# Branch sums, norms, residuals and gated products kept in PSUM banks, and a residual's bias added inside the feed-forward

## The chip, the cores and the metric

The kernel runs on one core of a Trainium2 chip. The metric is device time in microseconds (us) of one execution, with the median of several runs as the figure. A core has five engines that run in parallel, each with its own queue of instructions in a fixed order: PE (matrix products), VectorE (DVE in the profile), ScalarE (ACT), GpSimd (POOL) and SyncE (SP, which here only issues transfers). An instruction may wait on semaphores for others; whatever stands behind it on its engine then waits too. PE writes its products into PSUM, which the kernel uses as eight banks of 128 x 512 fp32; every other tile lies in SBUF.

## The reference

Two transformer blocks on 256 tokens of 1024 channels, all in fp32:

```
h = layer_norm(x)
proj = h @ w_in + b_in                      # q, k, v of two attentions, gates ga and gb
y_na  = neighbourhood_attention(...) @ w_branch_na
y_swa = windowed_gqa_with_sink(...) @ w_branch_swa
mixed = sigmoid(ga) * y_na + sigmoid(gb) * y_swa
h = layer_norm(ALPHA * h + mixed @ w_out + b_out)
u = square(relu(h @ w_ff1 + b_ff1))
h = layer_norm(ALPHA * h + u @ w_ff2 + b_ff2)
# second block, two layers
for layer in range(2):
    m = pool_mixer(rms_norm(x)) if layer == 0 else swa_sink_attention(rms_norm(x)) @ w_o
    x = x + rms_norm(m, mix_post_g)
    g, v = split(conv3(rms_norm(x) @ ffn_w_in))
    x = x + rms_norm((gelu(g) * v) @ ffn_w_out, ffn_post_g)
```

The pool mixer takes causal trailing means over 2, 4, 8 and 16 tokens minus the token itself, and a linear map per channel group. The convolution is causal, depthwise and three tokens wide.

## The kernel before

Every fp32 operand of a product is a pair of parts, a high one (the value in PE's fp32r format) and a low one (the rest). A product is three matmuls: high by high, low by high, high by low (`mm3`, L369). Weights stream through the core once, as chunks of 128 x 1024 (512 KB): SP loads a chunk into one of four `wraw` tiles, ACT writes its high part `whi` (L131), DVE its low part `wlo` (L141), and when DVE has done so SP may issue the next load. All 261 low parts of this kind are on DVE.

PSUM has two groups of four banks that rotate, `bank_a` and `bank_b`. A unit (`unit_a`) makes 256 output channels for all 256 tokens in two halves (m = 0 and 1); each half is a run of matmuls into the first 256 columns of the next `bank_a`, and an epilogue reads it. So the fourth half after a given one writes to the same bank, and PE must wait until the bank's last reader is done. `Acc` holds sums over many chunks in the four `bank_b` (two blocks of 128 tokens by two halves of 512 channels).

The order on every engine is the order in which the Python code issues instructions; nothing reorders it. The places that the change touches, in order of time:

- The branch stage (160 to 185 us). `y_swa` is made in four units of two halves, 12 matmuls a half. The epilogue `swa_epi` runs for each half i: DVE gated sum (L770, reads the bank), DVE `mix` (L772), ACT high part `mixh` (L775), a DVE `wlo` of the weights, DVE low part `mixl` (L777). Then comes the product with `w_out`.
- The first layer norms (`post_ln`, L290 to L284). DVE adds the residual to the bank and writes SBUF (`scr` is the name of those tiles), takes statistics there, centres, and scales.
- The entry of the feed-forward (205 to 237 us). The norm of tokens 128 to 255 is turned to feature-major and split (`to_fm`, `xl`), while PE runs three units for the first 128 tokens (`Tm.run`), whose outputs ACT copies (`tmc`). Right behind the second `xl`, DVE makes `h1 = ALPHA * h1 + b_ff2` for both token blocks (L907). `bff2` is one of four vectors that POOL loads then (L219).
- The feed-forward's loop, units 3 to 15: `ur` is relu (ACT, L889) and square (DVE, L890), `uh` and `ul` its parts; each turn also adds two chunks to the second product in `bank_b`.
- The pool stage (386 to 403 us). `pool_mm(0)` makes the mixer's output for tokens 0 to 127 in two `bank_b`. `resid_g` (L327) multiplies it by a gain, `sq_half` (ACT, L302) squares and sums it, `rms_rstd` (DVE `ve`, L307, then POOL) gives the inverse root, and `resid_add` (L331) adds the scaled product to X. In between `a_scale` (DVE, L952) scales the pooling matrix for tokens 128 to 255, on which `pool_fm(1)` on PE waits.
- The conv-GLU blocks (units 0 to 21, twice). For each half ACT and DVE make the convolution from the bank in an SBUF tile `cv` (L1085, L1086, L1088). After the second half ACT makes gelu in place in SBUF (L1092), DVE the product (L1093), and `split_out` the parts `ah` (ACT) and `al` (DVE). Units 0 to 2 are run ahead and finished between units 3, 4 and 5, through `bank_b`. From unit 6 on each turn also adds a chunk to the block's output. The residual chain behind a block is `resid_g`, `rms_rstd` and `resid_add` again.

Of the kernel before, what the change touches and what calls it, by code (L numbers as in the profile page):

```python
# [177 lines left out]
def model(tc, x_in, wts, bvec, cols_in, const_in, nab_in, pos_in, out):  # L178
    nc = tc.nc
    from contextlib import ExitStack  # L180
    with ExitStack() as top:
# [95 lines left out]
        def ln_centre(y, mr, g, q):  # L277
            s = HALF[q]
            nc.vector.scalar_tensor_tensor(out=y[:, s], in0=y[:, s], scalar=mr[0], in1=g[:, s],
                                           op0=ALU.subtract, op1=ALU.mult)  # L280

        def ln_out(y, mr, b, h, q):
            s = HALF[q]
            nc.vector.scalar_tensor_tensor(out=h[:, s], in0=y[:, s], scalar=mr[1], in1=b[:, s],  # L284
                                           op0=ALU.mult, op1=ALU.add)
# [1236 lines left out]
```

## Time and profile before

| | us |
|---|---|
| median of 3 runs | 884.81 (884.22 to 885.89) |
| the profiled execution | 879.9 |
| its span (first to last instruction) | 878.1 |
| PE busy | 836.4 (95%) |
| DVE busy | 631.0 (72%) |
| ACT busy | 492.0 (56%) |
| POOL busy | 146.0 (17%) |

The profile is of one execution, 879.9 us, of which 1.8 us lie around the span of 878.1. PE is busy in 95% of the span; its granted clock was 0.997 of full speed. Of the chain that ended last PE has 68%, DVE 16%, ACT 7%, 4% are issue and 3% transfers. A row of a timeline gives start, length and operation, and in brackets the idle time of that engine before it with what ended it. [...]

### The profile page before, as it was taken

How to read it: one execution, taken by the hardware profiler on the slowest of the kernel's cores; microseconds unless marked ns; L12 is line 12 of the kernel's file. 1: busy time of each engine (PE TensorE's matmuls, PEld its weight loads, DVE VectorE, ACT ScalarE, POOL GpSimd, SP SyncE). 2: the span in 40 equal slices, each digit the busy share in tenths (PEclk: the TensorE clock that was granted, in tenths of full speed). 3: DMA queues.
4: the chain of work that ended last, by engine and by line, in shares of the span. 5: the costliest groups of instructions: out<-in, count | busy, mean ns of one | idle time of the engine just before them, and what ended most of it. 6: DMA issues, size and time to landing. Idle time of an engine off the chain costs nothing.

```text
span 878.1 us, 15167 instructions
## 1 busy us (share of the span) xinstructions
PE 836.4 (95%) x5872; PEld 754.9 (86%) x5872; DVE 631.0 (72%) x1055; ACT 492.0 (56%) x905; POOL 146.0 (17%) x160
## 2 busy tenths in 40 slices
PE   4999999999899999898999999999999999999997
PEld 3878899979788999788999999988776999999995
DVE  4675684787838755777799777765696679977772
ACT  3464765544526555445677565465786566765551
POOL 0003000004999000311000000056720000000000
PEclk9999999999999999999999999999999999999999
DMA  7683364537636865533547655534153455766531
GB/s 265 201 305 106 137 196 135 174 124 241 217 97 199 295 227 192 177 111 121 178 149 268 194 183 205 191 117 137 53 189 120 145 192 186 250 213 208 175 121 48
DMA packets 43899, 154.61 MB, mean 176 GB/s; under 512 B 5010, under 2 KB 5906, under 8 KB 43827
## 3 DMA queue, kind: packets, MB, share of 16 engines
q1 hardware_dynamic: 41616, 146.90, 49.1%
q0 software_dynamic: 1632, 5.93, 2.1%
q8 instruction: 46, 0.75, 0.3%
q10 hardware_dynamic: 578, 0.82, 0.3%
q14 instruction: 27, 0.21, 0.1%
HBM read 152.58 MB, written 1.05 MB: 175 GB/s over the span
## 4 chain that ended last, share of the span: by engine, by line
PE 68%; DVE 16%; ACT 7%; issue 4%; DMA 3%; POOL 0%; SPq 0%; DVEq 0%; POOLq 0%; ACTq 0%
PE bank_a L369 36%; PE bank_b L369 24%; DVE wlo L141 7%; PE bank_a L424 4%; ACT whi L131 3%; DMA wraw<-wts_dram 2%; DVE p L1262 1%; DVE p L698 1%; ACT p L1274 1%; PE bank_a L348 1%; PE bank_a L720 1%; PE bank_b L709 1%; ACT scr L302 1%; DMA v<-bvec_dram 1%; PE bank_b L657 1%
## 5 line engine op out<-in xcount | busy, mean ns | idle before, releaser
L141 DVE TENSOR_TENSOR wlo<-wraw,whi 128x1024 fp32r<-128x1024 f32 x261 | 320.7, 1257 | 83.0 <-ACT whi L131 82.5
L369 PE MATMUL bank_a<-xh,whi 128*128 128x256 f32 x1056 | 295.9, 280 | 1.9 <-DVE cv L1088 1.7
L369 PE MATMUL bank_a<-xh,wlo 128*128 128x256 f32 x1056 | 292.7, 277 | 0.7 <-DVE wlo L141 0.5
L369 PE MATMUL bank_a<-xl,whi 128*128 128x256 f32 x1056 | 292.5, 277 | 0.0
L131 ACT ACTIVATE whi<-wraw 128x1024 fp32r<-128x1024 f32 x261 | 264.9, 1050 | 31.8 <-DMA wraw<-wts_dram 25.0
L369 PEld LDWEIGHTS bank_a<-xh,whi 128*128 128x128 f32 x1056 | 198.4, 188 | 7.3 <-ACT whi L131 2.7
L369 PEld LDWEIGHTS bank_a<-xl,whi 128*128 128x128 f32 x1056 | 198.7, 188 | 1.7
L369 PEld LDWEIGHTS bank_a<-xh,wlo 128*128 128x128 f32 x1056 | 198.4, 188 | 1.3 <-DVE wlo L141 1.3
L1085 ACT ACTIVATE cv<-bank_a,cols 128x256 f32<-128x256 f32 x76 | 41.9, 559 | 78.8 <-PE bank_a L369 78.8
L266 POOL TENSOR_TENSOR rstd<-ve,neghalf 128x1 f32<-128x1 f32 x22 | 13.4, 611 | 400.8 <-DVE ve L307 247.9
L369 PE MATMUL bank_b<-wlo,ah 128*128 128x512 f32 x176 | 69.3, 394 | 0.0
L369 PE MATMUL bank_b<-whi,al 128*128 128x512 f32 x176 | 69.0, 392 | 0.0
L369 PE MATMUL bank_b<-whi,ah 128*128 128x512 f32 x176 | 68.5, 389 | 0.0
L1086 DVE SCALAR_TENSOR_TENSOR cv<-bank_a,cols,cv 128x255 f32<-128x255 f32 x76 | 36.5, 481 | 41.9 <-ACT cv L1085 41.6
L869 POOL TENSOR_SCALAR wraw<-wraw,cols 128x256 f32<-128x256 f32 x28 | 29.7, 1079 | 166.1 <-DMA wraw<-wts_dram 162.4
L369 PE MATMUL bank_b<-whi,uh 128*128 128x512 f32 x128 | 50.3, 393 | 3.2 <-ACT uh L338 3.2
L369 PE MATMUL bank_b<-whi,ul 128*128 128x512 f32 x128 | 50.7, 396 | 2.5 <-DVE ul L339 2.5
L369 PE MATMUL bank_b<-wlo,uh 128*128 128x512 f32 x128 | 50.3, 393 | 0.0
L369 PEld LDWEIGHTS bank_b<-wlo,ah 128*128 128x128 f32 x176 | 33.1, 188 | 6.6
L1088 DVE SCALAR_TENSOR_TENSOR cv<-bank_a,cols,cv 128x254 f32<-128x254 f32 x76 | 36.6, 482 | 2.7
L369 PEld LDWEIGHTS bank_b<-whi,al 128*128 128x128 f32 x176 | 33.1, 188 | 6.3
L369 PEld LDWEIGHTS bank_b<-whi,ah 128*128 128x128 f32 x176 | 33.0, 188 | 6.0
(199 smaller groups left out, 1290.9 us busy)
## 6 DMA issues: line engine op xcount, KB each, us to landing
wraw<-wts_dram SPq DMA_DIRECT2D x268, 512.0 KB, 4.5
v<-bvec_dram POOLq DMA_DIRECT2D x10, 512.0 KB, 5.4
v<-bvec_dram SPq DMA_DIRECT2D x4, 512.0 KB, 7.1
nab<-nab_dram SPq DMA_DIRECT2D x4, 384.0 KB, 5.7
poolA<-const_dram POOLq DMA_DIRECT2D x1, 544.0 KB, 8.0
scr<-x_dram SPq DMA_DIRECT2D x2, 256.0 KB, 2.8
scr<-x_dram SPq DMA_DIRECT2D x1, 512.0 KB, 11.1
out_dram<-X SPq DMA_DIRECT2D x2, 256.0 KB, 2.1
```

The costliest lines, as they stand in the source:

```text
L131: self.nc.scalar.activation(out=hi, in_=r, func=AF.Copy)
L141: (eng or self.nc.vector).tensor_tensor(out=lo, in0=r, in1=hi.bitcast(F32), op=ALU.subtract)
L266: nc.gpsimd.tensor_tensor(out=r, in0=v, in1=neghalf, op=ALU.pow)
L302: nc.scalar.activation(out=junk[:, HALF[q if into is None else into]], in_=src, func=AF.Square, scale=1.0 / 32.0, accum_out=ss[:, q:q + 1])
L348: nc.tensor.transpose(out=b[:, j * P:(j + 1) * P], in_=h[:, k * P:(k + 1) * P], identity=ident)
L369: nc.tensor.matmul(o, lhsT=l, rhs=r, start=start and i == 0, stop=stop and i == 2)
L424: nc.tensor.matmul(o[:, :256], lhsT=self.kx(k)[b][:, t * P:(t + 1) * P], rhs=self.cs[u][k // 4][a][:, k % 4, :], start=i == 0 and k == 0, ...
L657: nc.tensor.matmul(s[e][:, j * T:(j + 1) * T], lhsT=q[r, j * P:(j + 1) * P], rhs=k[r, :], start=True, stop=True)
L869: nc.gpsimd.tensor_scalar(out=d, in0=d, scalar1=g, scalar2=None, op0=ALU.mult)
L1085: nc.scalar.activation(out=v, in_=o[:, :T], func=AF.Identity, scale=col(c + 2), bias=col(c + 3))
L1086: nc.vector.scalar_tensor_tensor(out=v[:, 1:T], in0=o[:, 0:T - 1], scalar=col(c + 1), in1=v[:, 1:T], op0=ALU.mult, op1=ALU.add)
L1088: nc.vector.scalar_tensor_tensor(out=v[:, 2:T], in0=o[:, 0:T - 2], scalar=col(c), in1=v[:, 2:T], op0=ALU.mult, op1=ALU.add)
```

## The change

Nothing of the arithmetic and no matmul is changed. Values that DVE and ACT kept in SBUF stay in the PSUM bank where PE left them, written over in place:

- `swa_epi` makes the gated sum and the mix in the half's `bank_a` columns; the low part `mixl` of half i is issued behind the sums of half i + 1.
- The layer norms behind `w_out` and behind the feed-forward add the residual, take statistics and centre in `bank_b`; only the last step writes SBUF. (The very first norm stays in SBUF.)
- `resid_g` writes its product over the `bank_b` it reads, and `resid_add` reads it there. In the pool stage the first `resid_g` stands in the code behind the squares instead of before them.
- The gelu and the gated product of a conv-GLU unit are made in columns 256 to 511 of the second half's `bank_a`, and `split_out` reads them there.
- `h1 = ALPHA * h1 + b_ff2` moves into units 12 and 13 of the feed-forward's loop, and the load of `bff2` to behind that of the pooling matrix on POOL's queue.

In the title's words "all low parts on VectorE" nothing differs from the kernel before.

```diff
...
-            nc.vector.scalar_tensor_tensor(out=y[:, s], in0=y[:, s], scalar=mr[0], in1=g[:, s],
+            nc.vector.scalar_tensor_tensor(out=y[q], in0=y[q], scalar=mr[0], in1=g[:, HALF[q]],
                                            op0=ALU.subtract, op1=ALU.mult)
...
-        def ln_stats(y, st, q, add=None, resid=None):
-            s = HALF[q]
-            if add is not None:
-                nc.vector.tensor_tensor(out=y[:, s], in0=add[q], in1=resid[:, s], op=ALU.add)
-            nc.vector.bn_stats(out=st[:, q, :], in_=y[:, s])
+        def ln_stats(y, st, q, resid=None):
+
+            if resid is not None:
+                nc.vector.tensor_tensor(out=y[q], in0=y[q], in1=resid[:, HALF[q]], op=ALU.add)
+            nc.vector.bn_stats(out=st[:, q, :], in_=y[q])
...
-        def resid_g(halves, g, junk, q):
+        def resid_g(halves, g, q):
+
+            nc.vector.tensor_tensor(out=halves[q], in0=halves[q], in1=g[:, HALF[q]], op=ALU.mult)
+
+        def resid_add(r, x, halves, q):
             s = HALF[q]
-            nc.vector.tensor_tensor(out=junk[:, s], in0=halves[q], in1=g[:, s], op=ALU.mult)
-
-        def resid_add(r, x, junk, q):
-            s = HALF[q]
-            nc.vector.scalar_tensor_tensor(out=x[:, s], in0=junk[:, s], scalar=r, in1=x[:, s],
+            nc.vector.scalar_tensor_tensor(out=x[:, s], in0=halves[q], scalar=r, in1=x[:, s],
                                            op0=ALU.mult, op1=ALU.add)
...
             def epi(m, o):
                 i = 2 * u + m
                 g, z = gate["gb", i], gate["ga", i]
-                nc.vector.scalar_tensor_tensor(out=g, in0=g, scalar=1.0, in1=o[:, :T], op0=ALU.add, op1=ALU.mult)
-                s = rot(apool, [P, T], F32, "mix", "mix", 2)
-                nc.vector.tensor_tensor(out=s, in0=g, in1=z, op=ALU.add)
+                s = o[:, :T]
+                nc.vector.scalar_tensor_tensor(out=s, in0=g, scalar=1.0, in1=s, op0=ALU.add, op1=ALU.mult)
+                nc.vector.tensor_tensor(out=s, in0=s, in1=z, op=ALU.add)
                 hi = rot(gpool, [P, T], F32R, "ga", "mixh", 8)
                 lo = rot(gpool, [P, T], F32R, "gb", "mixl", 8)
                 nc.scalar.activation(out=hi, in_=s, func=AF.Copy, scale=0.5)
                 mixed[i] = (hi, lo)
-                return [lambda: nc.vector.scalar_tensor_tensor(out=lo, in0=s, scalar=0.5, in1=hi.bitcast(F32),
-                                                               op0=ALU.mult, op1=ALU.subtract)]
+                if i:
+                    mix_low.pop()()
+                mix_low.append(lambda: nc.vector.scalar_tensor_tensor(
+                    out=lo, in0=s, scalar=0.5, in1=hi.bitcast(F32), op0=ALU.mult, op1=ALU.subtract))
             return epi
 
+        mix_low = []
         for u in range(4):
             unit_a(lambda k: att[4 + k], swa_epi(u), 4, ahead=1)
+        mix_low.pop()()
 
 
         ctx_x.close()
...
         tm = Tm(kx, 3, fpool)
         post_ln(acc, 1, x_t[1], g1, b1, h1[1])
         pscale = vec(V_PSCALE)
-        bff2 = vec(V_BFF2)
         g2 = vec(V_G2)
         b2 = vec(V_B2)
         tm.run(0)
         to_fm(h1[1], xT1, 1)
-        for t in range(2):
-            nc.vector.scalar_tensor_tensor(out=h1[t], in0=h1[t], scalar=ALPHA, in1=bff2, op0=ALU.mult, op1=ALU.add)
         tm.run(1)
         rope_angles()
         ctx_p = ExitStack()
         ppool = ctx_p.enter_context(tc.tile_pool(name="mixer", bufs=1, side="right"))
         poolA = ppool.tile([P, 4, N_POOL // 4], F32, name="poolA")
         nc.gpsimd.dma_start(out=poolA.rearrange("p a c -> p (a c)"), in_=const_in[:, K_POOL:K_POOL + N_POOL])
+        bff2 = vec(V_BFF2)
         mixpost0 = vec(V_MIXPOST0, None, late, "bx", 1)
         acc = Acc(32)
         for u in range(3, 16):
...
             unit_a(kx, ff1_epi(u))
+            if u in (12, 13):
+                nc.vector.scalar_tensor_tensor(out=h1[u - 12], in0=h1[u - 12], scalar=ALPHA, in1=bff2, op0=ALU.mult,
+                                               op1=ALU.add)
...
             sq_half(X[1][:, HALF[q]], j1, ss2[1], q)
         nc.scalar.activation(out=cb, in_=fb[1][:, :P], func=AF.Copy)
-        resid_g(accp.b[0], mixpost0, j0, 0)
         for q in range(2):
             sq_half(accp.b[0][q], j0, ss0, q, 1)
+        resid_g(accp.b[0], mixpost0, 0)
         lows = W.highs(2)
         r1 = rms_rstd(ss2[1])
         a_scale(1, r1)
         r0 = rms_rstd(ss0)
-        resid_g(accp.b[0], mixpost0, j0, 1)
+        resid_g(accp.b[0], mixpost0, 1)
         fb = pool_fm(1, cb)
         lows[0]()
         for q in range(2):
-            resid_add(r0, X[0], j0, q)
+            resid_add(r0, X[0], accp.b[0], q)
...
                     if m == 1:
-                        nc.scalar.activation(out=got[0], in_=got[0], func=AF.Gelu_apprx_tanh)
-                        nc.vector.tensor_tensor(out=v, in0=v, in1=got[0], op=ALU.mult)
+                        y = o[:, T:2 * T]
+                        nc.scalar.activation(out=y, in_=got[0], func=AF.Gelu_apprx_tanh)
+                        nc.vector.tensor_tensor(out=y, in0=v, in1=y, op=ALU.mult)
                         hi = rot(fp, [P, T], F32R, "ah", "ah", 8)
                         lo = rot(fp, [P, T], F32R, "al", "al", 8)
                         a_t[u] = (hi, lo)
-                        return [lambda: split_out(v, hi, lo)]
+                        return [lambda: split_out(y, hi, lo)]
...
```

The remaining places only pass the bank instead of the SBUF tile.

On DVE in the branch stage the kernel before has, from half 0 on (`gb` and `ga` are the gates, `mixl` the low part):

```order
L770 SCALAR_TENSOR_TENSOR gb<-gb,bank_a 128x256
L772 TENSOR_TENSOR mix<-gb,ga 128x256
L141 TENSOR_TENSOR wlo<-wraw,whi 128x1024
L777 SCALAR_TENSOR_TENSOR mixl<-mix,mixh 128x256
L770 SCALAR_TENSOR_TENSOR gb<-gb,bank_a 128x256
L772 TENSOR_TENSOR mix<-gb,ga 128x256
L141 TENSOR_TENSOR wlo<-wraw,whi 128x1024
L777 SCALAR_TENSOR_TENSOR mixl<-mix,mixh 128x256
```

and the changed kernel:

```order
L770 SCALAR_TENSOR_TENSOR bank_a<-gb,bank_a 128x256
L771 TENSOR_TENSOR bank_a<-bank_a,ga 128x256
L141 TENSOR_TENSOR wlo<-wraw,whi 128x1024
L770 SCALAR_TENSOR_TENSOR bank_a<-gb,bank_a 128x256
L771 TENSOR_TENSOR bank_a<-bank_a,ga 128x256
L778 SCALAR_TENSOR_TENSOR mixl<-bank_a,mixh 128x256
L141 TENSOR_TENSOR wlo<-wraw,whi 128x1024
L770 SCALAR_TENSOR_TENSOR bank_a<-gb,bank_a 128x256
L771 TENSOR_TENSOR bank_a<-bank_a,ga 128x256
```

The sums are in `bank_a`, and the first `mixl` stands behind the second half's sums, so that it is one half late from there on.

On DVE at the entry of the feed-forward the kernel before has (`v_2301` is `bff2`, `scr` the tiles of h1):

```order
L284 SCALAR_TENSOR_TENSOR scr<-scr,rstd,v_1336 128x512 x2
L339 TENSOR_TENSOR xl<-bank_a,xh 128x4x128 x2
L907 SCALAR_TENSOR_TENSOR scr<-scr,v_2301 128x1024 x2
L141 TENSOR_TENSOR wlo<-wraw,whi 128x1024 x6
L890 TENSOR_TENSOR ur<-ur 128x256
L339 TENSOR_TENSOR ul<-ur,uh 128x256
```

and the changed kernel, there and then in unit 12 of the loop (`v_2573` is `bff2`):

```order
L283 SCALAR_TENSOR_TENSOR scr<-bank_b,rstd,v_1336 128x512 x2
L338 TENSOR_TENSOR xl<-bank_a,xh 128x4x128 x2
L141 TENSOR_TENSOR wlo<-wraw,whi 128x1024 x6
L893 TENSOR_TENSOR ur<-ur 128x256
L338 TENSOR_TENSOR ul<-ur,uh 128x256
```

```order
L893 TENSOR_TENSOR ur<-ur 128x256
L141 TENSOR_TENSOR wlo<-wraw,whi 128x1024 x2
L338 TENSOR_TENSOR ul<-ur,uh 128x256
L924 SCALAR_TENSOR_TENSOR scr<-scr,v_2573 128x1024
L141 TENSOR_TENSOR wlo<-wraw,whi 128x1024 x2
L893 TENSOR_TENSOR ur<-ur 128x256
```

The two long operations are gone from between `xl` and `wlo`, and one of them stands between `ul` and a pair of `wlo` in unit 12; the other stands likewise in unit 13.

On DVE in the pool stage, with what each waits for, the kernel before has (`v_2585` is the gain, the two `ve` belong to tokens 128 to 255 and 0 to 127):

```order
L327 TENSOR_TENSOR scr<-bank_b,v_2585 128x512 [waits DMASW6_49,DMASW4_49,PE_49]
L307 SCALAR_TENSOR_TENSOR ve<-ss 128x1 [waits Activation_49]
L952 TENSOR_SCALAR poolA<-poolA,rstd 128x4x128 [waits Pool_49]
L307 SCALAR_TENSOR_TENSOR ve<-ss 128x1 [waits Activation_49]
L327 TENSOR_TENSOR scr<-bank_b,v_2585 128x512 [waits PE_49]
```

and the changed kernel:

```order
L326 TENSOR_TENSOR bank_b<-bank_b,v_2575 128x512 [waits DMASW6_49,PE_49,Activation_49]
L306 SCALAR_TENSOR_TENSOR ve<-ss 128x1
L956 TENSOR_SCALAR poolA<-poolA,rstd 128x4x128 [waits Pool_49]
L306 SCALAR_TENSOR_TENSOR ve<-ss 128x1 [waits Activation_49]
L326 TENSOR_TENSOR bank_b<-bank_b,v_2575 128x512 [waits PE_49]
```

The place in the queue is the same. The first `resid_g` now waits for ACT as well, and the `ve` behind it needs no wait of its own.

PE's and ACT's instructions stand in the same order as before. On PE the second halves of conv-GLU units 5, 6 and 7 and the branch stage's halves 4 to 7 wait for a later instruction of DVE than before.

## Rows read from the trace of the kernel before

**Rows 1.** Page, part 1: busy us, share of the span and instructions by engine.

```profile
PE 836.4 (95%) x5872; PEld 754.9 (86%) x5872; DVE 631.0 (72%) x1055; ACT 492.0 (56%) x905; POOL 146.0 (17%) x160
```

**Rows 2.** Windows: us, busy PE, PEld, DVE, ACT, POOL; clock, DMA share, GB/s.

```profile
445.00:570.00 125.00, 125.00 (x917) 117.59 (x916) 100.26 (x153) 74.18 (x116) 0.00 (x0) 1.00 0.59 202
```

**Rows 3.** Waits of PE: released by; us in all, times, longest.

```profile
PE bank_b L369 <- ACT uh L338: 3.2, 2, 2.3
...
PE bank_a L369 <- DVE cv L1088: 1.7, 2, 1.0
```

**Rows 4.** Groups by form: busy us, mean ns of one, idle before it.

```profile
L339 DVE TENSOR_TENSOR al<-cv,ah 128x256 fp32r<-128x256 f32 x44 | 18.5, 421 | 2.9 <-ACT ah L338 2.9
...
L339 DVE TENSOR_TENSOR ol<-bank_a,oh 128x256 fp32r<-128x256 f32 x16 | 6.7, 419 | 2.8 <-ACT oh L338 2.8
...
L302 ACT ACTIVATE scr<-X 128x512 f32<-128x512 f32 x16 | 10.1, 631 | 20.8 <-DVE X L284 12.2 <-DVE X L331 8.5
...
L302 ACT ACTIVATE scr<-bank_b 128x512 f32<-128x512 f32 x16 | 9.6, 598 | 22.6 <-PE bank_b L369 22.5
```

**Rows 5.** DVE in the branch stage: start us, us, operation, idle before.

```profile
164.40 0.41 DVE L770 SCALAR_TENSOR_TENSOR gb<-gb,bank_a 128x256 f32<-128x256 f32 x1
...
165.19 1.22 DVE L141 TENSOR_TENSOR wlo<-wraw,whi 128x1024 fp32r<-128x1024 f32 x1
...
166.33 0.42 DVE L777 SCALAR_TENSOR_TENSOR mixl<-mix,mixh 128x256 fp32r<-128x256 f32 x1
166.66 0.41 DVE L770 SCALAR_TENSOR_TENSOR gb<-gb,bank_a 128x256 f32<-128x256 f32 x1
...
174.81 0.42 DVE L777 SCALAR_TENSOR_TENSOR mixl<-mix,mixh 128x256 fp32r<-128x256 f32 x1 [0.48 <-ACT mixh L775]
```

**Rows 6.** PE after each wait in the branch stage and after it.

```profile
171.66 0.39 PE L369 MATMUL bank_a<-oh,whi 128*128 128x256 f32 x1 [0.51 <-DVE gb L770]
...
182.74 0.50 PE L369 MATMUL bank_b<-whi,mixh 128*128 128x512 f32 x1 [0.46 <-ACT whi L131]
...
184.00 0.50 PE L369 MATMUL bank_b<-wlo,mixh 128*128 128x512 f32 x1 [0.52 <-DVE wlo L141]
```

**Rows 7.** DVE, ACT and PE at the entry of the feed-forward, DVE inside it.

```profile
211.14 2.36 DVE L907 SCALAR_TENSOR_TENSOR scr<-scr,v 128x1024 f32<-128x1024 f32 x2 [2.51 <-DMA v<-bvec_dram]
...
213.42 5.03 DVE L141 TENSOR_TENSOR wlo<-wraw,whi 128x1024 fp32r<-128x1024 f32 x4
...
210.80 2.00 ACT L131 ACTIVATE whi<-wraw 128x1024 fp32r<-128x1024 f32 x2
...
224.36 0.49 PE L369 MATMUL bank_b<-whi,uh 128*128 128x512 f32 x1 [2.31 <-ACT uh L338]
...
325.43 0.42 DVE L890 TENSOR_TENSOR ur<-ur 128x256 f32<-128x256 f32 x1 [2.32 <-ACT ur L889]
```

**Rows 8.** DVE, ACT and PE in the pool stage.

```profile
391.29 0.68 DVE L327 TENSOR_TENSOR scr<-bank_b,v 128x512 f32<-128x512 f32 x1
...
392.16 0.16 DVE L307 SCALAR_TENSOR_TENSOR ve<-ss 128x1 f32<-128x1 f32 x1 [0.19 <-ACT scr L302]
...
392.98 0.49 DVE L952 TENSOR_SCALAR poolA<-poolA,rstd 128x512 f32<-128x512 f32 x1 [0.66 <-POOL rstd L266]
...
394.50 0.16 DVE L307 SCALAR_TENSOR_TENSOR ve<-ss 128x1 f32<-128x1 f32 x1 [1.03 <-ACT scr L302]
...
393.54 0.20 ACT L302 ACTIVATION_READ_ACCUMULATOR scr<-bank_b 128x1 f32 x1
...
398.65 0.39 PE L369 MATMUL bank_b<-whi,xl 128*128 128x256 f32 x1 [1.01 <-DVE xl L339]
```

**Rows 9.** DVE and PE at unit 6 of the first conv-GLU block.

```profile
445.29 0.42 DVE L339 TENSOR_TENSOR al<-cv,ah 128x256 fp32r<-128x256 f32 x1
...
441.77 0.36 PE L369 MATMUL bank_a<-xh,whi 128*128 128x256 f32 x1 [0.76 <-DVE cv L1088]
...
442.32 0.28 PE L369 MATMUL bank_a<-xl,whi 128*128 128x256 f32 x1
```

More of the change, by code (lines that the diff above doesn't have):

```diff
@@ L283, in ln_out @@
             s = HALF[q]
-            nc.vector.scalar_tensor_tensor(out=h[:, s], in0=y[:, s], scalar=mr[1], in1=b[:, s],
+            nc.vector.scalar_tensor_tensor(out=h[:, s], in0=y[q], scalar=mr[1], in1=b[:, s],
                                            op0=ALU.mult, op1=ALU.add)
-        def ln_stats(y, st, q, add=None, resid=None):
-            s = HALF[q]
-            if add is not None:
-                nc.vector.tensor_tensor(out=y[:, s], in0=add[q], in1=resid[:, s], op=ALU.add)
-            nc.vector.bn_stats(out=st[:, q, :], in_=y[:, s])
+        def ln_stats(y, st, q, resid=None):
+            if resid is not None:
+                nc.vector.tensor_tensor(out=y[q], in0=y[q], in1=resid[:, HALF[q]], op=ALU.add)
+            nc.vector.bn_stats(out=st[:, q, :], in_=y[q])
         def layer_norm(y, mr, g, b, h, mid=lambda: None):
@@ L497, in ln0 @@
             for q in range(2):
-                ln_stats(x_t[t], st, q)
+                ln_stats(halved(x_t[t]), st, q)
             mr = ln_rstd(st)
             mid()
-            layer_norm(x_t[t], mr, g0, b0, x_t[t], mid2)
+            layer_norm(halved(x_t[t]), mr, g0, b0, x_t[t], mid2)
         ln0(0, lambda: lows.pop(0)())
@@ L795, in post_ln @@
             for q in range(2):
-                ln_stats(y, st, q, acc.b[t], y)
-            layer_norm(y, ln_rstd(st), g, b, h)
+                ln_stats(acc.b[t], st, q, y)
+            layer_norm(acc.b[t], ln_rstd(st), g, b, h)
         acc = Acc(8)
@@ L934, in a_stats @@
                 st2[t] = small([P, 2, 6], "bst")
-            ln_stats(h1[t], st2[t], q, acc.b[t], h1[t])
+            ln_stats(acc.b[t], st2[t], q, h1[t])
         def a_centre(t):
@@ L939, in a_centre @@
             for q in range(2):
-                ln_centre(h1[t], mr2[t], g2, q)
+                ln_centre(acc.b[t], mr2[t], g2, q)
         def a_norm(t):
@@ L945, in a_norm @@
             for q in range(2):
-                ln_out(h1[t], mr2[t], b2, X[t], q)
+                ln_out(acc.b[t], mr2[t], b2, X[t], q)
                 sq_half(X[t][:, HALF[q]], junk, ss2[t], q)
@@ L991, in mid_a @@
                 fm_split(fb[0], dT, 0, (q,))
-                ln_centre(h1[1], mr2[1], g2, q)
+                ln_centre(acc.b[1], mr2[1], g2, q)
         ffnpre0 = vec(V_FFNPRE0)
@@ L1016, in resid_rms @@
                 if q == 0:
-                    resid_g(halves, gpost, junk, q)
+                    resid_g(halves, gpost, q)
             r = rms_rstd(ss)
-            resid_g(halves, gpost, junk, 1)
+            resid_g(halves, gpost, 1)
             for q in range(2):
-                resid_add(r, X[t], junk, q)
+                resid_add(r, X[t], halves, q)
         def pre_rms(t, g, h):
@@ L1034, in model @@
         for q in range(2):
-            ln_out(h1[1], mr2[1], b2, X[1], q)
+            ln_out(acc.b[1], mr2[1], b2, X[1], q)
         for q in range(2):
@@ L1067, in model @@
         for q in range(2):
-            resid_g(accp.b[1], mixpost0, j1, q)
+            resid_g(accp.b[1], mixpost0, q)
         for q in range(2):
-            resid_add(r1, X[1], j1, q)
+            resid_add(r1, X[1], accp.b[1], q)
         h0 = pre_rms(1, ffnpre0, j1)
@@ L1135, in l1_chain @@
                 if q == 0:
-                    resid_g(acc.b[t], gpost, j, q)
+                    resid_g(acc.b[t], gpost, q)
             r = rms_rstd(ss)
-            resid_g(acc.b[t], gpost, j, 1)
+            resid_g(acc.b[t], gpost, 1)
             lows = W.highs(2 - t)
             for q in range(2):
-                resid_add(r, X[t], j, q)
+                resid_add(r, X[t], acc.b[t], q)
             ss = small([P, 2], "ss")
```

1 line of the change is left out of this document (removed).

## The prediction

> **What bounds the kernel now.** I read the busy times first: PE works in 836.4 of the span's 878.1 us, DVE in 631.0 [rows 1]. So an edit counts only where it changes one of PE's idle moments, which make 878.1 - 836.4 = 41.7 us in all. The table of windows says where they are not: in the conv-GLU block from 445 to 570 us PE is busy for 125.00 of 125.00 us, while DVE has 100.26 and ACT 74.18 [rows 2]. Forty-odd DVE and ACT operations that change their memory there cost nothing as long as no bank comes too late. PE's waits, read third, name the seams between the stages: 2.3 us on `uh` at the entry of the feed-forward, 1.7 us in two waits on `cv` at the entries of the conv-GLU blocks [rows 3]. The timelines around the seams, read last, carry the sum. What counts at each seam is which instruction frees the bank or makes the operand that PE waits for.
>
> **The operand's memory.** By the diff 176 DVE operations get another memory on one side (24 in the branch stage, 32 in the norms, 32 in the residuals, 88 in the gated products), and 88 of ACT's. Reading costs DVE the same: 421 ns for `al` from SBUF, 419 for `ol` from a bank [rows 4]. ACT is quicker by 33 ns with a bank as its source, 598 against 631 ns [rows 4]. No row shows DVE or ACT writing a bank. The nearest difference by memory is ACT's 33 ns, so I bound a write at 33 ns less or more; I take 0, the value of DVE's own rows.
>
> [...]
>
> **1. Branch stage.** DVE paces it: one half takes it 166.66 - 164.40 = 2.26 us (gated sum, mix, `wlo`, `mixl`) [rows 5], PE's 12 matmuls only about 1.4. PE needs for half i + 4 the bank of half i. Before, that is free after the gated sum; PE's last half started at 171.66 after a wait of 0.51 [rows 6]. Now the bank is held until `mixl`, and that stands one half later. For half 0: the sums of half 1 take the old place of `mixl`, 166.33, and need 165.19 - 164.40 = 0.79 us; `mixl` then runs from 167.12 to 167.54 [rows 5]. With the unchanged cycle `mixl` of half 3 ends at 167.54 + 3 x 2.26 = 174.3, and PE's last half starts at 174.4 instead of 171.66: 2.7 us later. Behind it stands the product with w_out, and there two waits were paid, 0.46 on `whi` and 0.52 on `wlo` [rows 6]. They go, since PE comes 2.7 us later, and DVE itself is quicker: `mixl` waited 0.48 us for ACT's `mixh` in each of two halves without a `wlo` in between [rows 5], and one half later `mixh` is long done. Net 2.7 - 0.98 = **+1.75**. Bounds: +2.7 if neither wait goes; -1.5 (0.51 + 0.46 + 0.52 all gone) if the banks should come in time after all.
>
> **2. Entry of the feed-forward.** Behind `xl` DVE waits 2.51 us for `bff2`, spends 2.36 on h1, and starts on the `wlo` at 213.42 [rows 7]. Now the first `wlo` can start when its `whi` is there: ACT begins two at 210.80, so the first is ready at 210.80 + 1.05 = about 211.9. That is 1.55 us earlier. The loads of the fifth and sixth chunk are issued when the first two `wlo` end, so they, the last `wlo`, `ur` and `uh` move up as well. PE waited 2.31 us for that `uh` [rows 7]; it keeps about 0.75. The term is **-1.55**; bounds 0 (a load that does not come earlier) and -3.2 (all waits on `uh` [rows 3]). The two moved operations, 1.2 us each, stand in units 12 and 13, where DVE waits 2.32 us for `ur` once in a turn [rows 7]: 0. Without that cover they would cost up to 2.4. The load of `bff2` now stands behind that of the pooling matrix on POOL's queue, turns ahead of its use: 0.
>
> **3. Pool stage.** Before, the first `resid_g` ran at 391.29 while DVE waited for the squares of X anyway; then `ve` at 392.16, `a_scale` at 392.98, and with it PE's `pool_fm(1)` [rows 8]. Now `resid_g` overwrites the bank that ACT is squaring, so it waits for ACT's read, which ends at 393.54 + 0.20 = 393.74 [rows 8]. `ve` is queued behind it: `resid_g` 393.76 to 394.44, `ve` at 394.4, so 2.2 us late, and `a_scale` and PE with it, at 395.2. Some of this was idle time in any case: PE waited 1.01 us for `xl` at 398.65 [rows 8], and on the way from `ve` to that `xl` DVE itself idled, 1.03 us ahead of the second `ve` alone [rows 8]. With the 0.15 us or so that it idled for `whi` behind it, `xl` comes 2.2 - 1.15 = 1.05 us later, and PE with it: **+1.05**, with 0 and +2.2 as bounds.
>
> **4. Entries of the conv-GLU blocks.** The second half of unit 6 takes the bank of the second half of unit 4. That was free after `cv` (L1088); now `split_out` holds it until `al`, which ends at 445.29 + 0.42 = 445.71 [rows 9]. PE starts unit 6 at 441.77 and wants the bank 24 matmuls later; its starts settle at 0.12 us apart (the fifth at 442.32), so at about 444.7 [rows 9]. A wait of 1.0 us, in each of the two blocks: **+2.0**. Bounds: 0 (if `al` came a us earlier) and +2.4. Later units don't pay: a bank is wanted again after two whole turns, in each of which PE also adds a chunk to the output, and the full windows [rows 2] leave nothing to be given back.
>
> **5. The rest.** The norms and residuals only change operands: 32 and 32 operations, mostly beside PE. `resid_g` in the other chains waited for ACT's squares before as well. 0, with 0.3 either way.
>
> **The sum.** 1.75 - 1.55 + 1.05 + 2.0 = +3.25 us. Against the profiled execution that is 879.9 + 3.25 = 883.2; that execution is 4.9 us below the median of the runs, so on the median 884.81 + 3.25 = **888.1**.
>
> **Rivals.**
> A. Faster: DVE's queue, rid of three stalls, runs so early that the banks come in time. It is one mechanism, a lead of DVE, and it decides if `mixl` of half 3 ends before 171.7 and `al` of unit 4 before 444.7. Then the branch stage gives -1.5, the feed-forward's entry -1.55, the conv-GLU entries 0, and the pool stage keeps its +1.05, since ACT sets it: -2.0, 882.8. For it: DVE works in only 631 of 878 us and could catch up. Against it: PE's need lies 2.7 and 1.0 us ahead of the ends that I work out, and DVE runs without a gap there.
>
> B. No change: the holds bite, but ACT's shorter gelu and `ah` and DVE's shorter queue take half off each of the three: +4.8 becomes +2.4, less 1.55 is +0.85, 885.7.
>
> C. Dearer bank operands: 33 ns more (ACT's difference by memory, with the other sign) on each of the three DVE operations of a half, in four halves, and on some seven operations ahead of `al`, `a_scale` and `xl`: 19 x 0.033 = 0.6, 888.7. Against it stands the pair 419 and 421 ns.
>
> [...]
>
> D. The two moved operations lose their cover: if `wlo` in units 12 and 13 reaches PE too late, up to 2.4 on top, 890.5. Against it: 2.32 us of idle time in each turn.
>
> **Chances.** My forecast 0.5; A 0.16; B 0.2; C 0.08; D 0.06. A measurement of this kernel tells a change from none at about 0.2%, 1.8 us. The forecast's own range is 886 to 890, so some 0.08 of its chance falls within 0.2%, as do 0.18 of B's and 0.02 of A's: faster 0.14, same 0.28, slower 0.58. For 8 in 10 the range goes from 883.0, which takes in B and leaves out most of A, to 890.6, which takes in C and D.
>
> **What would show it.** In the changed profile: the waits of PE on `mixl` (L778) in halves 4 to 7, the last of them ended at about 174.4; no wait of DVE on `bff2`, and PE's wait on `uh` near 224 cut to under 1 us; `resid_g` of the pool stage started at ACT's end, and `pool_fm(1)` 2.2 us later against its predecessor; PE waits of about 1 us on `al` at the second half of unit 6 in both blocks. I would be wrong if PE's waits at those two entries are missing, if DVE's operations with a bank as target take other than 0.42 us for 256 columns, or if a stall of DVE that I removed comes back at the next weight chunk. Of the four terms the pool stage is the least certain, since there I follow three engines through seven steps.

## The result, and the profile after

| | before | changed |
|---|---|---|
| median, us | 884.51 (880.32 to 885.89, 4 runs) | 894.43 (893.08 to 895.77, 4 runs) |
| profiled execution, us | 879.9 | 895.45 |
| span, us | 878.1 | 893.7 |

The ratio is 1.0124, with a 95% interval of 1.0083 to 1.0166: slower by some 10 us where I forecast 3.25, and above the range's end of 890.6. The sign was right, the size was not.

The first part of the page of the changed kernel, beside [rows 1]:

```profile
PE 844.0 (94%) x5872; PEld 762.0 (85%) x5872; DVE 630.4 (71%) x1055; ACT 490.8 (55%) x905; POOL 145.9 (16%) x160
```

PE's idle time grew from 41.7 to 893.7 - 844.0 = 49.7 us, and its busy time by 7.6 us for the same matmuls, which ran at a lower clock or a slower rate in some stretches (both in the last section). The waits of PE in the changed kernel (released by; us in all, times, longest), beside [rows 3]:

```profile
PE bank_a L368 <- DVE al L338: 7.4, 5, 2.1
PE bank_a L368 <- DVE cv L1092: 3.4, 2, 1.8
PE bank_a L368 <- DVE mixl L778: 3.0, 4, 1.3
PE bank_a L977 <- DVE poolA L956: 2.9, 1, 2.9
...
PE bank_b L368 <- ACT uh L337: 1.5, 2, 0.9
```

The wait on `uh` is down from 3.2 to 1.5 us, `mixl` and `poolA` are new or longer, as forecast. But `al` holds PE five times and not twice, for 7.4 us and not 2.0, and the waits on `cv` have doubled. PE's timeline after these waits (start, length, operation, idle before it):

```profile
174.34 0.39 PE L368 MATMUL bank_a<-oh,whi 128*128 128x256 f32 x1 [0.57 <-DVE mixl L778]
...
223.79 0.50 PE L368 MATMUL bank_b<-whi,uh 128*128 128x512 f32 x1 [0.61 <-ACT uh L337]
...
394.08 2.08 PE L977 MATMUL bank_a<-poolA,X 128*128 128x128 f32 x8 [2.89 <-DVE poolA L956]
...
439.42 0.39 PE L368 MATMUL bank_a<-xh,whi 128*128 128x256 f32 x1 [1.08 <-DVE al L338]
...
444.18 0.36 PE L368 MATMUL bank_a<-xh,whi 128*128 128x256 f32 x1 [1.67 <-DVE cv L1092]
...
449.22 0.38 PE L368 MATMUL bank_a<-xh,whi 128*128 128x256 f32 x1 [2.06 <-DVE al L338]
```

The first row answers to 171.66 of [rows 6], the second to 224.36 of [rows 7], the third to the scaled pooling matrix of [rows 8], the last three to the entry of the first conv-GLU block [rows 9]: a wait of 1.08 at unit 5, 1.67 instead of 0.76 at unit 6, and 2.06 at its second half.

Comparing the start of the same ACT operations in both traces shows where the time is lost. The changed kernel is 1.1 us behind at 200 us, 0.3 ahead at 360, level at 410, 6.2 behind at the end of the first conv-GLU block and 15.6 behind at the end of the second. So the three other seams, together with a gain at 368 us that I had not forecast (e6 below), gave nothing in sum, and nearly all of it was lost in and around the two conv-GLU blocks. What happens in one is seen on ACT. First unit 3 of the first block in the kernel before:

```profile
433.06 0.55 ACT L1085 ACTIVATE cv<-bank_a,cols 128x256 f32<-128x256 f32 x1
433.50 0.41 ACT L1092 ACTIVATE cv<-cv 128x256 f32<-128x256 f32 x1
433.81 1.06 ACT L131 ACTIVATE whi<-wraw 128x1024 fp32r<-128x1024 f32 x1
435.89 0.42 ACT L338 ACTIVATE ah<-cv 128x256 fp32r<-128x256 f32 x1 [1.02 <-DVE cv L1093]
```

and in the changed kernel:

```profile
434.02 0.56 ACT L1089 ACTIVATE cv<-bank_a,cols 128x256 f32<-128x256 f32 x1
436.40 0.39 ACT L1097 ACTIVATE bank_a<-cv 128x256 f32<-128x256 f32 x1 [1.81 <-DVE cv L1092]
436.73 1.05 ACT L131 ACTIVATE whi<-wraw 128x1024 fp32r<-128x1024 f32 x1
437.68 0.36 ACT L337 ACTIVATE ah<-bank_a 128x256 fp32r<-128x256 f32 x1
```

Before, gelu (L1092) follows the second half's first convolution step at once, at 433.50, while DVE still has the other two steps ahead of it (434.33 and 434.85). (Neighbouring rows of ACT and of DVE overlap by some 0.1 us: the first row ends at 433.06 + 0.55 = 433.61, the second starts at 433.50.) Now gelu (L1097) waits 1.81 us for DVE's last convolution step on the second half. It needs nothing from it, but writes to the bank that the step reads. Not even the columns are the same: gelu writes 256 to 511, the step reads the first 256. The wait goes by the bank, as PE's waits of 1.08 and 2.06 us on `al` do, where PE writes the first 256 columns and `al` reads the others; with the other half's bank as its target gelu has no such wait (e3 below). The `whi` that had followed gelu is late as well, and DVE, which has to come back for the product, for `wlo` and for `al`, now idles in between (DVE, changed kernel):

```profile
435.83 0.48 DVE L1092 SCALAR_TENSOR_TENSOR cv<-bank_a,cols,cv 128x254 f32<-128x254 f32 x1
436.82 0.43 DVE L1098 TENSOR_TENSOR bank_a<-cv,bank_a 128x256 f32<-128x256 f32 x1 [0.52 <-ACT bank_a L1097]
437.81 1.23 DVE L141 TENSOR_TENSOR wlo<-wraw,whi 128x1024 fp32r<-128x1024 f32 x1 [0.55 <-ACT whi L131]
438.95 0.42 DVE L338 TENSOR_TENSOR al<-bank_a,ah 128x256 fp32r<-128x256 f32 x1
```

The `al` of the first two finished units, first in the kernel before, then in the changed one (DVE):

```profile
431.78 0.42 DVE L339 TENSOR_TENSOR al<-cv,ah 128x256 fp32r<-128x256 f32 x1 [0.48 <-ACT ah L338]
...
440.17 0.43 DVE L339 TENSOR_TENSOR al<-cv,ah 128x256 fp32r<-128x256 f32 x1 [0.48 <-ACT ah L338]
```

```profile
432.76 0.42 DVE L338 TENSOR_TENSOR al<-bank_b,ah 128x256 fp32r<-128x256 f32 x1 [0.45 <-ACT ah L337]
...
442.58 0.42 DVE L338 TENSOR_TENSOR al<-bank_b,ah 128x256 fp32r<-128x256 f32 x1 [0.45 <-ACT ah L337]
```

From one to the next (a finished unit and a whole one) it was 440.17 - 431.78 = 8.39 us before and is 442.58 - 432.76 = 9.82 now: 1.43 more. The second such pair of the block loses the same (8.37 before, 9.80 now).

### The profile page after: what moved, and what is told of

The parts are those of the page before. It is cut to its first block, busy times and chain, and to the rows that moved or that the text cites. A ratio compares the mean times of both kernels' runs of the same rounds, so it can differ in the third digit from the quotient of the medians.

```text
span 893.7 us, 15090 instructions
## 1 busy us (share of the span) xinstructions
PE 844.0 (94%) x5872; PEld 762.0 (85%) x5872; DVE 630.4 (71%) x1055; ACT 490.8 (55%) x905; POOL 145.9 (16%) x160
## 3 DMA queue, kind: packets, MB, share of 16 engines
HBM read 152.58 MB, written 1.05 MB: 172 GB/s over the span
## 4 chain that ended last, share of the span: by engine, by line
PE 68%; DVE 15%; ACT 8%; issue 3%; DMA 3%; POOL 1%; DVEq 0%; SPq 0%; POOLq 0%; ACTq 0%
PE bank_a L368 34%; PE bank_b L368 24%; DVE wlo L141 7%; PE bank_a L423 5%; ACT whi L131 3%; DMA wraw<-wts_dram 2%; PE bank_a L347 1%; DVE p L1267 1%; DVE p L697 1%; ACT p L1279 1%; PE bank_a L719 1%; DVE cv L1092 1%; PE bank_b L708 1%; DVE cv L1090 1%; PE bank_b L656 1%
## 5 line engine op out<-in xcount | busy, mean ns | idle before, releaser
L1089 ACT ACTIVATE cv<-bank_a,cols 128x256 f32<-128x256 f32 x76 | 41.9, 562 | 49.8 <-PE bank_a L368 49.7
L1097 ACT ACTIVATE bank_a<-cv 128x256 f32<-128x256 f32 x38 | 14.8, 388 | 64.8 <-DVE cv L1092 64.8
L1092 DVE SCALAR_TENSOR_TENSOR cv<-bank_a,cols,cv 128x254 f32<-128x254 f32 x76 | 36.6, 482 | 2.7
```

The source lines that it names most:

```text
L1089: nc.scalar.activation(out=v, in_=o[:, :T], func=AF.Identity, scale=col(c + 2), bias=col(c + 3))
L1092: nc.vector.scalar_tensor_tensor(out=v[:, 2:T], in0=o[:, 0:T - 2], scalar=col(c), in1=v[:, 2:T], op0=ALU.mult, op1=ALU.add)
L1097: nc.scalar.activation(out=y, in_=got[0], func=AF.Gelu_apprx_tanh)
```

## The experiments

Two theories of the loss in the conv-GLU blocks stood against each other. Theory 1: gelu's new target makes ACT wait for DVE, so that the two run in series while the blocks start up. Theory 2: the bank's longer hold, until `al`, is all of it, as I had forecast, and merely mis-sized.

**e1_glu_sbuf.** The gated product back in SBUF, all else as changed:

```diff
-                        y = o[:, T:2 * T]
-                        nc.scalar.activation(out=y, in_=got[0], func=AF.Gelu_apprx_tanh)
-                        nc.vector.tensor_tensor(out=y, in0=v, in1=y, op=ALU.mult)
+                        nc.scalar.activation(out=got[0], in_=got[0], func=AF.Gelu_apprx_tanh)
+                        nc.vector.tensor_tensor(out=v, in0=v, in1=got[0], op=ALU.mult)
...
-                        return [lambda: split_out(y, hi, lo)]
+                        return [lambda: split_out(v, hi, lo)]
```

> The changed kernel with the gated product of the conv-GLU units back in SBUF (gelu in place in cv, product in cv), all else as changed. Theory 1 (gelu, which now writes into the bank of the unit's second half, has to wait until VectorE has read that bank twice for the convolution, so ScalarE, VectorE and the banks run in series at the start of each block): PE's waits on al go (7.4 us to 0), its waits on cv fall from 3.4 to about 1.7 us, no stretch of half clock near 450 us; time about 884.5, within 2 us of the kernel before, since the other three terms gave about 0 together by 420 us. Theory 2 (only the longer hold of the bank until al): the same figures. A rival, that the other edits cost several us: 887 or more.

Measured: 882.48 us where the kernel before had 880.63 on the same chip, ratio 1.0015 (0.9989 to 1.0041). There is no wait on `al`; the waits on `cv` are 1.4 us. Gelu and the gated product make all of the loss that can be measured; what is left lies between 1 us faster and 3.6 us slower. Both theories had said so: this run places the loss and does not choose between them.

**e2_glu_only.** The kernel before with the same lines as changed:

```diff
-                        nc.scalar.activation(out=got[0], in_=got[0], func=AF.Gelu_apprx_tanh)
-                        nc.vector.tensor_tensor(out=v, in0=v, in1=got[0], op=ALU.mult)
+                        y = o[:, T:2 * T]
+                        nc.scalar.activation(out=y, in_=got[0], func=AF.Gelu_apprx_tanh)
+                        nc.vector.tensor_tensor(out=y, in0=v, in1=y, op=ALU.mult)
```

> The kernel before with only the conv-GLU edit (gelu and gated product in the bank of the second half). Theories 1 and 2: the whole loss of the change, 892 to 896 us, with PE waits on al of about 7 us and on cv of 3.4. If the loss needs the other edits too, less than 890.

Measured: 894.36, ratio 1.0144 (1.0107 to 1.0182). PE's waits in the first block:

```profile
441.80 0.39 PE L369 MATMUL bank_a<-xh,whi 128*128 128x256 f32 x1 [1.36 <-DVE al L339]
...
446.55 0.36 PE L369 MATMUL bank_a<-xh,whi 128*128 128x256 f32 x1 [1.76 <-DVE cv L1088]
...
451.60 0.39 PE L369 MATMUL bank_a<-xh,whi 128*128 128x256 f32 x1 [1.98 <-DVE al L339]
...
461.41 0.39 PE L369 MATMUL bank_a<-xh,whi 128*128 128x256 f32 x1 [1.31 <-DVE al L339]
```

The edit alone costs what the whole change costs. By the starts of the same ACT operations it loses 6.0 us in either block (2.5 behind at 427 us, 8.5 at 578; 9.8 at 671, 15.8 at 860). Up to 427 us its code is that of the kernel before: the 2.5 us there are the scatter between single executions.

**e3_gelu_first_bank.** The changed kernel with gelu into the bank of the first half, which nobody reads any more by then:

```diff
+                    if m == 0:
+                        got[2] = o
                     if m == 1:
                         y = o[:, T:2 * T]
-                        nc.scalar.activation(out=y, in_=got[0], func=AF.Gelu_apprx_tanh)
-                        nc.vector.tensor_tensor(out=y, in0=v, in1=y, op=ALU.mult)
+                        z = got[2][:, T:2 * T]
+                        nc.scalar.activation(out=z, in_=got[0], func=AF.Gelu_apprx_tanh)
+                        nc.vector.tensor_tensor(out=y, in0=v, in1=z, op=ALU.mult)
```

> The changed kernel with gelu writing to the bank of the unit's FIRST half (columns 256 to 511), the product still in the bank of the second half. Theory 1: gelu starts right after the first half's convolution again (ScalarE's wait of 1.8 us on cv ahead of gelu goes), but the first half's bank is now held until the product, which before ended 2.4 us later than PE wanted the bank at unit 6: a PE wait of about 3 us at the first half of unit 6 in each block and none at the second; sum of PE's waits in a block about 3.5 instead of 5; time 888 to 891. Theory 2: the waits on al stay at about 7 us, 893 or more.

Measured: 888.02, ratio 1.0081 (1.0053 to 1.0109). The waits of PE on the product, then two of them on its timeline, and gelu on ACT's:

```profile
PE bank_a L368 <- DVE bank_a L1101: 6.3, 4, 2.6
```

```profile
435.46 0.39 PE L368 MATMUL bank_a<-xh,whi 128*128 128x256 f32 x1 [0.71 <-DVE bank_a L1101]
...
443.80 0.38 PE L368 MATMUL bank_a<-xh,whi 128*128 128x256 f32 x1 [2.62 <-DVE bank_a L1101]
```

```profile
432.58 0.57 ACT L1089 ACTIVATE cv<-bank_a,cols 128x256 f32<-128x256 f32 x1
433.03 0.39 ACT L1100 ACTIVATE bank_a<-cv 128x256 f32<-128x256 f32 x1
```

Gelu (L1100) starts at 433.03, right behind the second half's first convolution step, with no wait. The waits on `al` are gone, and PE waits for the product (L1101) instead, 2.62 us at unit 6 and 0.71 at unit 5 in the first block: 3.3 where I expected about 3.5. The second half's bank is held until `al` as in the changed kernel, and the time is that of theory 1. The missing waits on `al` alone would not settle it, since PE comes later to the second half after its wait at the first, which covers a hold of the second bank. The next run has no such cover.

**e4_gelu_sbuf.** The changed kernel with gelu in place in SBUF; the product and the split behind it stay in the second half's bank, held until `al`:

```diff
-                        nc.scalar.activation(out=y, in_=got[0], func=AF.Gelu_apprx_tanh)
-                        nc.vector.tensor_tensor(out=y, in0=v, in1=y, op=ALU.mult)
+                        nc.scalar.activation(out=got[0], in_=got[0], func=AF.Gelu_apprx_tanh)
+                        nc.vector.tensor_tensor(out=y, in0=v, in1=got[0], op=ALU.mult)
```

> The changed kernel with gelu in place in SBUF and only the product (and the split behind it) in the bank of the second half. Theory 1: gelu no longer waits for the second half's convolution; what is left is the hold until al, which I worked out as about 1.0 us at unit 6 in each block: PE's waits on al 2 to 2.5 us in all, time 886 to 888. Theory 2: as the changed kernel, waits on al about 7 us, 893 or more.

Measured: 885.47, ratio 1.0045 (1.0023 to 1.0067). PE's waits on `al`, all of them:

```profile
445.46 0.39 PE L368 MATMUL bank_a<-xh,whi 128*128 128x256 f32 x1 [1.00 <-DVE al L338]
...
728.45 0.38 PE L368 MATMUL bank_a<-xh,whi 128*128 128x256 f32 x1 [1.02 <-DVE al L338]
```

1.00 and 1.02 us, one at unit 6 of each block: the term that I had worked out is there to the tenth, and theory 2 fails: with the hold unchanged, 2.0 of the 7.4 us are left. (The time is 0.5 us under the range I gave.) The run differs from the changed kernel in gelu's target alone, and that is worth 1.0124 - 1.0045 = 0.8%, some 7 us; the two ratios are known to 0.4% and 0.2%.

**e5_branch_only, e8_pool_only.** The kernel before with the branch stage's edit alone, and with the pool stage's first `resid_g` alone in the bank and behind the squares, each run once. The branch stage's lines are those of the change; the pool stage's:

```diff
-        resid_g(accp.b[0], mixpost0, j0, 0)
         for q in range(2):
             sq_half(accp.b[0][q], j0, ss0, q, 1)
+        y0 = accp.b[0][0]
+        nc.vector.tensor_tensor(out=y0, in0=y0, in1=mixpost0[:, HALF[0]], op=ALU.mult)
```

> The kernel before with only the branch stage's edit (sums and mix in the bank, mixl one half late). My theory, from the trace of the changed kernel: PE waits on mixl four times (1.3, 0.6, 0.6, 0.6 us), its last half starts at about 174.4, the waits on whi and wlo near 183 go, so the stage's net loss is 1 to 1.8 us; the first norm's PE-released operations come 1 to 1.8 us later than before. Rival (the loss is given back by the next wait of the feed-forward's entry): no shift left behind 224 us.

> The kernel before with only the first residual product of the pool stage made in the bank, behind the squares. My theory: it waits for ScalarE's read, PE's wait on poolA grows from 0.7 to about 2.9 us, the wait on xl behind it goes, so the stage ends 1 to 1.6 us later. Rival (hidden by the next seam at 402 us, where PE waits for the norm): no shift at the transposition that starts near 402.

PE in the branch stage of the first, and PE at the scaled pooling matrix in the second:

```profile
174.33 0.38 PE L369 MATMUL bank_a<-oh,whi 128*128 128x256 f32 x1 [0.58 <-DVE mixl L779]
```

```profile
395.91 2.08 PE L973 MATMUL bank_a<-poolA,X 128*128 128x128 f32 x8 [2.88 <-DVE poolA L952]
```

The branch stage is 1.1 us behind at 200 us, at the low end of what I expected (1.75 in the prediction): PE's last half comes 2.7 late as worked out and the two later waits are gone. The missing 0.6 us is in the price of those two waits. PE's rows around them in the kernel before, beside the two of [rows 6]:

```profile
181.88 0.40 PE L369 MATMUL bank_b<-wlo,mixh 128*128 128x512 f32 x1
...
183.08 0.40 PE L369 MATMUL bank_b<-whi,mixl 128*128 128x512 f32 x1
...
184.33 0.39 PE L369 MATMUL bank_b<-whi,mixh 128*128 128x512 f32 x1
184.56 0.40 PE L369 MATMUL bank_b<-whi,mixl 128*128 128x512 f32 x1
```

Without a wait, starts lie 0.23 us apart (184.33 to 184.56). From 181.88 over 182.74, 183.08 and 184.00 to 184.33 they lie 0.86, 0.34, 0.92 and 0.33 apart, so that the two waits cost 2.45 - 4 x 0.23 = 1.53 us of starts, where the idle times in brackets make 0.98. And 2.7 - 1.53 is 1.15. The rival fails too: at 224 us the run is still 1.3 behind.

The pool stage loses 1.65 us between 385 and 410 us (1.05 in the prediction, 1 to 1.6 expected), and nothing of it is hidden at 402 us. The windows from 390 to 402 us (PE, PEld, DVE, ACT, POOL, then the clock, DMA share and GB/s) of the kernel before, of this run, and of e1, which has the same edit here:

```profile
390.00:402.00 12.00, 9.94 (x70) 9.34 (x69) 9.17 (x16) 8.13 (x18) 1.64 (x3) 0.86 0.14 47
```

```profile
390.00:402.00 12.00, 9.12 (x61) 9.02 (x60) 7.46 (x14) 8.15 (x18) 1.64 (x3) 0.72 0.17 58
```

```profile
390.00:402.00 12.00, 8.62 (x59) 8.20 (x58) 8.39 (x15) 7.36 (x16) 1.65 (x3) 0.86 0.12 44
```

The granted clock has a mean of 0.72 in this run instead of 0.86. Windows of 0.5 us show what such means are made of in the kernel before (0.86) and in the changed one (0.72): the clock reads 1.00 or 0.50, with other values only in the windows where it changes, and it stays at 0.50 for some 3.4 us in the former (394.4 to 397.8) and some 6.8 in the latter (391.8 to 398.6). Five traces have this edit, all with the same wait of 2.9 us on `poolA`. In the changed kernel, e3 and this run the clock's mean is 0.72 and the stage costs 1.6 to 1.7 us; in e1 and e4 it is 0.86, as in the kernel before, and the stage costs 1.0 and 1.2. The three traces with the lower mean thus lose 0.4 to 0.7 us more than the two others, which agree with the 1.05 that I had worked out. I put that down to the clock, which no run tests by itself; the length of the wait does not decide whether it comes.

**e6_bias_move_only.** The kernel before with the bias of the second residual moved:

```diff
-        for t in range(2):
-            nc.vector.scalar_tensor_tensor(out=h1[t], in0=h1[t], scalar=ALPHA, in1=bff2, op0=ALU.mult, op1=ALU.add)
...
+            if u in (12, 13):
+                nc.vector.scalar_tensor_tensor(out=h1[u - 12], in0=h1[u - 12], scalar=ALPHA, in1=bff2, op0=ALU.mult,
+                                               op1=ALU.add)
```

> The kernel before with only the bias of the second residual moved into units 12 and 13, and its load behind the pooling matrix. My theory: PE's wait on uh near 224 falls from 2.3 to about 0.7 us, nothing is paid in units 12 and 13; 1.6 us faster, 0.2%, at the edge of what five rounds can tell. Rival (the lead is lost again at the next seam): the same time, with a longer PE wait at 237 or 368 us.

Measured: 877.73 us against 881.74, ratio 0.9962 (0.9944 to 0.9981). PE's wait on `uh` is 0.74 us:

```profile
222.01 0.49 PE L369 MATMUL bank_b<-whi,uh 128*128 128x512 f32 x1 [0.74 <-ACT uh L338]
```

From 200 to 222 us it gains 1.6, as forecast, but the medians differ by 4.0, more than the 1.6 that I expected, and the interval (1.7 to 4.9 us) leaves that value just outside. The profile of the kernel before is a favourable one at this seam. Here PE waited 2.31 us for `uh` [rows 7]; e2, e5 and e8, which have the same code at this place, give (one row of each):

```profile
225.27 0.51 PE L369 MATMUL bank_b<-whi,uh 128*128 128x512 f32 x1 [3.76 <-ACT uh L338]
```

```profile
225.68 0.50 PE L369 MATMUL bank_b<-whi,uh 128*128 128x512 f32 x1 [2.63 <-ACT uh L338]
```

```profile
224.52 0.80 PE L369 MATMUL bank_b<-whi,uh 128*128 128x512 f32 x1 [4.18 <-ACT uh L338]
```

The six traces with the bias moved have 0.3 to 0.74 there. By ACT's starts from 200 to 222 us those six gain 1.6 to 1.8 us on the profile of the kernel before, while e5, e2 and e8 lose 0.3, 1.4 and 1.8 on it. Measured against these four executions the move is worth 1.6 to 3.6 us.

This run gains another 1.5 at 368 us, where PE waits for `ul`: 1.0 us instead of 2.5. In the kernel before that low part ran beside POOL's scaling of a weight chunk and took DVE 1.48 us; here, as in the changed kernel, POOL is done when it starts, and it takes 0.41:

```profile
366.47 1.48 DVE L339 TENSOR_TENSOR ul<-ur,uh 128x256 fp32r<-128x256 f32 x1
```

```profile
360.50 7.17 POOL L858 TENSOR_TENSOR wraw<-wraw,v 128x512 f32<-128x512 f32 x4 [14.25 <-DMA wraw<-wts_dram]
```

```profile
365.95 0.41 DVE L338 TENSOR_TENSOR ul<-ur,uh 128x256 fp32r<-128x256 f32 x1
```

```profile
358.53 6.41 POOL L861 TENSOR_TENSOR wraw<-wraw,v 128x512 f32<-128x512 f32 x4 [11.91 <-DVE ur L893]
```

These are DVE and POOL of the kernel before, then of the changed kernel. The ten traces fall into two kinds: 1.48 us in the five where this `ul` starts before POOL's end (before, e2, e3, e7, e8), 0.41 in the five where it starts behind it (changed, e1, e4, e5, e6). It does not go with the bias: e3 and e7 have it moved and take 1.48, e5 has not and takes 0.41.

**e7_best.** The changed kernel with the gated product and the branch stage as before, and the pool stage's first `resid_g` in SBUF ahead of the squares as before; norms, the other residuals and the bias as changed:

```diff
-        for q in range(2):
-            sq_half(accp.b[0][q], j0, ss0, q, 1)
-        resid_g(accp.b[0], mixpost0, 0)
+        j2 = [j0[:, HALF[0]], accp.b[0][1]]
+        nc.vector.tensor_tensor(out=j2[0], in0=accp.b[0][0], in1=mixpost0[:, HALF[0]], op=ALU.mult)
+        for q in range(2):
+            sq_half(accp.b[0][q], j0, ss0, q, 1)
```

> The pieces that did not lose: norms and residuals in banks and the bias moved, as changed; the branch stage and the gated products as before; in the pool stage the first residual product goes to SBUF ahead of the squares, as before. My theory: -1.6 at the feed-forward's entry, the rest 0: 879 where before is 880.6, ratio 0.997 to 1.000, with PE waits on mixl and al absent, and on poolA 0.7. Rival (norms and residuals in banks cost something on the chains between the stages): 1.000 to 1.003.

Measured: 878.41, ratio 0.9961 (0.9946 to 0.9976). PE's waits on `mixl` and `al` are absent, that on `poolA` is 0.7. The gain is a little more than the range that I gave, as in e6. The run beats both kernels, and it and e6 can't be told apart: norms and residuals in banks neither gain nor lose anything beyond the 0.2% that either ratio is known to.

## Why the prediction was wrong

- What bounds the kernel: right. PE's waits at the seams decide, and the steady loops are full (PE 90.00 of 90.00 us from 750 to 840 us).
- The operand's memory: right. A write to a bank I had taken at 0, from no row that showed one; the runs fill that in. With a bank as target, in the changed kernel, DVE took 693 ns for the residual's sum (685 with SBUF, in the kernel before), 695 for `resid_g` (686), 430 for the gated product (426): 4 to 9 ns, where I had bounded 33. ACT's gelu was quicker, 388 instead of 411 ns. Rival C is out: `al` took 417 ns from `bank_a` and 421 from SBUF.
- Term 1, branch stage, +1.75: the mechanism is there wait for wait (the last half at 174.34, forecast 174.4); measured +1.1. I had priced the two waits that go by their idle time, 0.98 us; by the starts of the matmuls around them they cost 1.53 (e5).
- Term 2, feed-forward, -1.55: measured -1.6 against the profile that I had worked from. That it meets the forecast is partly luck: against other executions of the same code it is up to -3.6, and the medians of e6 give -4.0 with all that follows from the move (e6). The two operations in units 12 and 13 cost nothing: e6 is 2.35 us ahead at 240 us and at 360.
- Term 3, pool stage, +1.05: the wait on `poolA` grew by 2.2 as worked out. Measured 1.0 and 1.2 in the two traces where the clock's mean was 0.86 as before, 1.6 to 1.7 in the three where it was 0.72, among them the changed kernel's; the clock was not in the sum.
- Term 4, entries of the conv-GLU blocks, +2.0: **this step failed.** It measured 12 us in e2's trace (6.0 in each block); by the ratios of the changed kernel and e1 it is 1.0124 - 1.0015 = 1.1%, some 10 us. I weighed one end of the bank's life, when it becomes free again (1.0 us in each block, confirmed by e4), and took for granted that gelu starts as before: operations that change their memory "cost nothing as long as no bank comes too late" for PE. I did not ask what the writer of a bank must wait for; my list of instructions that wait for a later one than before had PE's halves and not ACT's gelu. Gelu's data come from the first half, but its target is the second half's bank, so it starts after DVE's last read of that one, 1.81 us after ACT was free at unit 3; rival B had even counted gelu as a gain, for ACT's shorter time. The serial step costs 1.43 us in each pair of units, and as I read it DVE and ACT pace the start of the block, so PE pays: in the changed kernel's first block it is 1.3 us late behind the wait at unit 5, 4.6 behind those at unit 6, and 6.2 behind a stretch at a granted clock of 0.50 that follows (last section).
- Term 5: right, as far as e7 can tell.
- Rivals: the faster one (A) fell as expected, the holds bite. The event that did come, a new wait on another engine ahead of the hold, was none of the four.

## What to carry to other kernels

The two results that were moved into a bank which others still read waited here for their last read: gelu 1.81 us for DVE's convolution step at unit 3, the pool stage's first `resid_g` 2.32 us for ACT's squares (DVE's L326 at 392.11 in the changed kernel). So for each new target ask who used it last, not only who wants it next. A dependency of that kind doesn't show in the order of instructions or in the kinds of their waits, where the gelu waited for DVE before and after; it shows when one writes down which of DVE's operations it is. And idle time on DVE and ACT over the whole span (29% and 45% in the changed kernel) says nothing about a start-up of a few units: at the entry of the first conv-GLU block PE waited 1.08 + 1.67 + 2.06 = 4.81 us for DVE.

## What the runs showed of the hardware that I had not expected

A stretch of lower clock stands in one trace where another has a wait. In the changed kernel PE, after 2.06 us idle at 449.22, ran at a granted clock of 0.50 from 450 to 452 us (windows of the changed kernel, columns as above):

```profile
448.00:450.00 2.00, 0.78 (x6) 0.78 (x7) 1.97 (x5) 0.76 (x2) 0.00 (x0) 0.95 0.09 25
450.00:452.00 2.00, 2.00 (x11) 2.00 (x11) 1.38 (x4) 0.43 (x2) 0.00 (x0) 0.50 0.63 252
```

In e2 the clock stayed at 1.00 there, and PE waited 1.31 us more at 461.41 instead. Both lost about 6 us in the block. I read that as DVE and ACT setting the pace, so that a slower PE costs nothing more; no run tests it by itself.

PE's matmuls ran at two rates at a granted clock of 1.00. From 750 to 840 us the kernel before and the changed one have (windows, one of each):

```profile
750.00:840.00 90.00, 90.00 (x659) 84.60 (x659) 71.51 (x107) 53.86 (x83) 0.00 (x0) 1.00 0.61 209
```

```profile
750.00:840.00 90.00, 90.00 (x640) 84.36 (x639) 70.52 (x106) 53.74 (x82) 0.00 (x0) 1.00 0.60 205
```

659 and 640 matmuls in the same 90 us, all of them busy: 114 against 118 ns between starts of 256 columns. The slower rate took the second block of the changed kernel's profile, of e4 and of e6, and not that of the other seven traces; over 125 us it makes 3 to 4 us. It is in the 9.4 us by which the changed kernel falls back from the end of the first block to that of the second, where e2 has 6.0 in its block. What sets the rate I did not find. Together with the wait for `uh` (2.3 to 4.2 us with the same code) it is one reason why single executions of one kernel differ by several us. The two profiles differ by 15.6 us and the medians by 9.9, since the profiled execution of the kernel before lies 4.6 us below its median and that of the changed kernel 1.0 above. Stages are therefore compared here by the starts of the same instructions, and even these carry the scatter of one execution.
